# Squared-ReLU MLP of a two-layer decoder: half-width weight loads in the first pass, a third raw tile, and one ring of result tiles

## The chip, the core and the metric

The kernel runs on one core of a Trainium2 chip. The core has a matrix engine (TensorE, PE), whose weight loads are a stream of their own (PEld), a vector engine (VectorE, DVE), a scalar engine (ScalarE, ACT), a general engine (GpSimd, POOL) and a queue engine (SyncE, SP) that here only issues loads. Operands lie in SBUF, 128 partitions wide; PE writes its sums into PSUM banks of 128 x 512 floats. Every engine takes its own instructions strictly in program order and waits on semaphores for what other engines or transfers have to deliver. The metric is the device time of one execution in microseconds (us), less is better. "L76" is line 76 of the kernel of before; where a line of the changed kernel is meant, the text says so.

## The reference

A residual stream of 1024 tokens by 1024 features passes two layers: a token mixer (layer 0 latent attention, layer 1 a gated linear recurrence), then an MLP, all in 32-bit floats. The change touches the first matrix product of the MLP alone, `h @ w1`, and the squared ReLU behind it:

```python
def sq_relu_mlp(h, w1, w2):          # h (1024, 1024), w1 (1024, 4096), w2 (4096, 1024)
    a = jax.nn.relu(h @ w1)
    return (a * a) @ w2

for layer in range(DEPTH):           # DEPTH = 2
    ...
    h = h + rms_norm(m, norm_gains[layer, 1])
    a = rms_norm(h, norm_gains[layer, 2])
    h = h + rms_norm(sq_relu_mlp(a, mlp_w1[layer], mlp_w2[layer]), norm_gains[layer, 3])
```

## The kernel before, in words

**Numbers in two halves.** A 32-bit operand is kept as a rounded high part and the rest. `split` (L74 to L77) makes them: ACT copies the high part (L76), then DVE subtracts it from the source (L77). `mm3` (L79 to L83) multiplies two such operands with three matmuls: high by high, high by low, low by high.

**The product in 16 pairs.** `mlp_up` (L703 to L871) treats `h @ w1` as a product of 2 x 2 blocks with seven block products instead of eight, and additions before and after. The stream h lies in SBUF as four quarters, B11, B12, B21 and B22, of 512 features by 512 tokens each. The 4096 columns of w1 fall into 16 pairs p of 256 columns; a pair has two halves of 128 columns, and each of them an upper and a lower half of the 1024 rows. One block product is 4 x 3 = 12 matmuls of 128 x 512 into one PSUM bank. The seven products of a pair are:

- `first_two` (L787): the first columns' upper rows by B11, copied by ACT to the tile sP1 (L793)
- `add_second` (L796): the first columns' lower rows by B21, added in the same bank; ReLU and square on ACT (L784, L785) make the result h11
- `others` (L803): the five products with T2 (into the bank `tr`), T1 (bank `mm`), T3 (bank `c`), B22 (added to the T1 bank) and T4 (added to the T3 bank). T1 to T4 are sums and differences of the quarters of h, made by `tsums` (L722). Their weights are sums of the raw halves, which DVE makes (L806 to L810) and which are then split. Out of the banks DVE builds U = b + sP1 (L814), X5 (L821), h22, h12, h21 (L825, L828, L831), and after ReLU and square four more sums (L836 to L846)

Seven planes of results per pair are stored to the scratch `hsp` in DRAM by POOL's queue (`spill`, L781). The second matrix product, `mlp_down`, reads them from there.

**Two passes.** A first pass runs `first_two` and `add_second` alone for pairs 0 to 7 (EARLY = 8), while the last rows of the token mixer are still being finished: these two products need only B11 and B21, the others need the sums T1 to T4 of all quarters. `tc.high_priority` (L850) sets where the pass's instructions stand in each engine's order. It stores sP1 to the scratch `psp` (L853) and h11 to plane 0 of `hsp`. The main pass (L860) then loads both back for pairs 0 to 7 (L864, L866) and runs the five products left; for pairs 8 to 15 it runs all seven. One MLP half per layer, so all of this occurs twice.

**Loads.** `raw_half` (L767) brings a 128 x 4 x 256 piece of w1, the upper or the lower rows of both columns of a pair, 512 KB, into a raw tile, on SP's queue. Two raw tiles exist, one in the pool G0 and one in G, taken in turn by the count `own["n"]`. `w_parts` (L772) splits a raw piece or a sum into one of five weight tiles: every fifth by the count `own["w"]` is in G0, four are in G. In the first pass, each piece is loaded in full, and only its first 128 columns are split and used.

**Result tiles.** A 128 x 512 result takes one tile. In the first pass sP1 and h11 take two tiles `he` in G in turn. In the main pass `h512` (L761) gives out tiles: even draws from a ring `h` (9 tiles in layer 0, 6 in layer 1), odd draws from a ring `h2` (4 and 8) in a pool that is opened at L859. A pair draws eight; a tile is reused when its last reader, mostly the store, is done with it.

**Order.** The engines' orders are fixed before the run by a scheduler that places the instructions by priority and readiness; names like raw_920 carry running numbers of the tiles.

Of the kernel before, what the change touches and what calls it, by code (L numbers as in the profile page):

```python
# [11 lines left out]
F32 = mybir.dt.float32  # L12
# [9 lines left out]
P = 128  # L22
# [36 lines left out]
def trunk(ctx, tc, x, x_t, positions, norm_gains, mla_w_in, mla_q_norm, mla_kv_norm, mla_w_uq, mla_w_ukv, mla_w_o,  # L59
# [9 lines left out]
    def new(p, shape, dt, tag, bufs=None):  # L69
        uid[0] += 1  # L70
        kw = {} if bufs is None else {"bufs": bufs}
        return p.tile(shape, dt, tag=tag, name=f"{tag}_{uid[0]}", **kw)
# [630 lines left out]
    def mlp_up(layer):  # L703
# [3 lines left out]
        w1 = mlp_w1[layer].rearrange("(k p) c -> p k c", p=P)  # L707
        with tc.tile_pool(name=f"up{layer}", bufs=1, side="left", reuse_waits="tile") as wp:

            new(wp, [P, 512], F32, "h", 9 if layer == 0 else 6)  # L710
            new(wp, [P, 1024], F32, "s", 3)
            T2 = new(wp, [P, 2, 4, 512], F32R, "T2")
            T3 = new(wp, [P, 2, 4, 512], F32R, "T3")
            T4 = new(wp, [P, 2, 4, 512], F32R, "T4")

            B11, B12, B21, B22 = A[0, 0], A["whole"], A[1, 0], A[1, 1]
            T1 = A[0, 1] if (0, 1) in A else new(wp, [P, 2, 4, 512], F32R, "T1")
# [37 lines left out]
                for k in range(4):  # L755
                    mm3(ps, (w[:, 0, k], w[:, 1, k]), (X[:, 0, k], X[:, 1, k]), not more and k == 0, k == 3, more)

            hs = {"n": 0, "more": None}

            def h512():  # L760
                hs["n"] += 1  # L761
                if hs["more"] and hs["n"] % 2:
                    return new(hs["more"], [P, 512], F32, "h2", 4 if layer == 0 else 8)
                return new(wp, [P, 512], F32, "h", 9 if layer == 0 else 6)

            def raw_half(p, kh):
                own["n"] += 1  # L767
                r = new(G0 if own["n"] % 2 else G, [P, 1024], F32, "raw").rearrange("p (k c) -> p k c", c=256)
                SP.dma_start(r, w1[:, kh * 4:(kh + 1) * 4, p * 256:(p + 1) * 256])
                return r  # L770

            def w_parts(src):  # L772
                own["w"] = own.get("w", 0) + 1
                w = new(G0, [P, 2, 1024], F32R, "w", 1) if own["w"] % 5 == 0 else new(G, [P, 2, 1024], F32R, "w", 4)
                n = src.shape[1] * src.shape[2]
                v = w[:, :, :n].rearrange("p i (k c) -> p i k c", c=src.shape[2])
                split(v, src)
                return v
# [5 lines left out]
                ACT.activation(h, src, AF.Relu)  # L784
                ACT.activation(h, h, AF.Square)  # L785

            def first_two(p, rA, w12):  # L787

                wa = w_parts(rA[:, :, :P])
                a = new(PG, [P, 512], F32, "mm")  # L790
                product(a, wa, B11)
                sP1 = h512() if p >= EARLY else new(G, [P, 512], F32, "he", 2)
                ACT.activation(sP1, a, AF.Copy)  # L793
                return a, sP1
# [53 lines left out]

            for p in range(EARLY):
                with tc.high_priority(offset=AHEAD[layer]):  # L850
                    rA, rB = raw_half(p, 0), raw_half(p, 1)
                    a, sP1 = first_two(p, rA, None)
                    POOL.dma_start(psp[p * P:(p + 1) * P, :], sP1)  # L853
                    wb = w_parts(rB[:, :, :P])
                    add_second(p, a, wb)
            tsums()

            act["whole"].close()
# [1 line left out]
            for p in range(NP):  # L860
                rA, rB = raw_half(p, 0), raw_half(p, 1)
                if p < EARLY:
                    h11 = h512()
                    SP.dma_start(h11, hsp[0, p * P:(p + 1) * P, :])  # L864
                    sP1 = h512()
                    SP.dma_start(sP1, psp[p * P:(p + 1) * P, :])  # L866
                    others(p, rA, rB, w_parts(rB[:, :, P:]), sP1, h11)
                else:
                    a, sP1 = first_two(p, rA, None)
                    wb = w_parts(rB)  # L870
                    others(p, rA, rB, wb[:, :, :, P:], sP1, None, lambda: add_second(p, a, wb))  # L871

# [484 lines left out]
```

## Time and profile before

| | |
|---|---|
| median of 3 runs | 2400.32 us (2399.58 to 2401.26) |
| the profiled execution, its own time | 2396.59 us |
| its span, first to last instruction | 2394.9 us |
| mean granted clock of TensorE | 0.987 |
| mean DMA rate | 143 GB/s (341.51 MB) |
| ReLU of h11 out of the bank (L784, he<-mm) | 16 times, median 597 ns |

The span is that of one execution taken by the profiler; its own time has a little more around the span, and the median of the other runs lies 3.7 us above it. In the profile, a name is the tile that an instruction writes or reads: `raw` a piece of w1 as loaded, `w` a weight tile after the split, `s` a sum, `he`, `h`, `h2` the result tiles, `mm`, `tr`, `c` PSUM banks, `A` the quarters of h, `T` the tiles T1 to T4. A group's row gives line, engine, operation, out<-in with partitions x elements, the count, then busy time and mean nanoseconds of one, then the idle time of its engine just before, with what ended it. A row of the timeline gives start (us from the span's start), duration, engine, line and operation, and in brackets how long the engine had waited and for whom. A row of DMA issues gives the count, the size of one and the median time from issue to landing. In layer 0 the first pass lies at 480 to 545 us and pairs 0 to 7 of the main pass at 545 to 666; in layer 1 at 1720 to 1786 and 1786 to 1916.

### The profile page before, as it was taken

What the parts mean: (1) busy time and instruction counts of PE and PEld (TensorE: products, weight loads), DVE (VectorE), ACT (ScalarE), POOL (GpSimd) and SP (SyncE); (2) the same over time, 40 slices, a digit from 0 to 9 for tenths busy, and PEclk for the clock granted to TensorE, in tenths of its full rate; (3) what the DMA queues carried; (4) which work ended last, traced back from release to release, by engine and by line L of the source; (5) the groups of instructions that cost most, each with busy time, mean ns of one, the idle gap of its engine ahead of it and who ended that gap; (6) DMA issues with size and microseconds to landing.
All of it is one profiled execution on the core that took longest, in us unless ns stands there. A gap on an engine that the chain in (4) does not pass through costs nothing. (4 is left out here: it accounts for less than half of the span.)

```text
span 2394.9 us, 30791 instructions
## 1 busy us (share of the span) xinstructions
PE 2285.7 (95%) x11487; PEld 1918.8 (80%) x11487; DVE 1616.4 (67%) x2311; ACT 1170.9 (49%) x1908; POOL 355.5 (15%) x718
## 2 busy tenths in 40 slices
PE   9999999988899999998899999999978999999996
PEld 8889998866688878886788888888766788888885
DVE  5657884477676557578765667756777767467578
ACT  5445654363344454433575546754453445443443
POOL 1300000121121200001332213221211212100002
PEclk9999999999999999999999999999999999999998
DMA  6000002485554584554612333222455545663743
GB/s 216 27 27 10 10 10 90 157 267 164 172 184 151 187 299 133 190 181 149 219 45 88 106 105 116 83 77 80 150 184 187 200 149 172 214 238 132 257 138 141
DMA packets 229540, 341.51 MB, mean 143 GB/s; under 512 B 16999, under 2 KB 136846, under 8 KB 229390
## 3 DMA queue, kind: packets, MB, share of 16 engines
q1 hardware_dynamic: 205582, 259.84, 33.7%
q0 software_dynamic: 23808, 79.71, 9.0%
q8 instruction: 90, 1.47, 0.3%
q14 instruction: 60, 0.49, 0.1%
HBM read 255.61 MB, written 83.89 MB: 142 GB/s over the span
## 5 line engine op out<-in xcount | busy, mean ns | idle before, releaser
L77 DVE TENSOR_TENSOR w<-raw,w 128x1024 fp32r<-128x1024 f32 (+1 forms) x256 | 280.7, 1102 | 175.9 <-ACT w L76 174.9
L76 ACT ACTIVATE w<-raw 128x1024 fp32r<-128x1024 f32 (+1 forms) x256 | 240.7, 947 | 248.0 <-PE mm L83 82.1
L81 PE MATMUL mm<-A,w 128*128 128x512 f32 x832 | 330.9, 400 | 30.5 <-ACT he L784 12.8
L82 PE MATMUL mm<-A,w 128*128 128x512 f32 x832 | 329.7, 397 | 0.6 <-DVE A L77 0.5
L83 PE MATMUL mm<-A,w 128*128 128x512 f32 x832 | 327.9, 396 | 0.5 <-DVE w L77 0.5
L76 ACT ACTIVATE w<-s 128x1024 fp32r<-128x1024 f32 x156 | 165.1, 1058 | 318.6 <-PE c L83 107.0
L77 DVE TENSOR_TENSOR w<-s,w 128x1024 fp32r<-128x1024 f32 x156 | 190.6, 1222 | 143.2 <-ACT w L76 142.7
L81 PEld LDWEIGHTS mm<-A,w 128*128 128x128 f32 x832 | 158.4, 191 | 72.5 <-ACT he L784 16.1
L145 POOL TENSOR_TENSOR rstd<-rstd,nhalf 128x1 f32<-128x1 f32 x56 | 56.3, 1008 | 964.9 <-DVE rstd L144 939.0
L83 PEld LDWEIGHTS mm<-A,w 128*128 128x128 f32 x832 | 158.7, 191 | 34.2 <-DVE w L77 1.0
L82 PEld LDWEIGHTS mm<-A,w 128*128 128x128 f32 x832 | 158.4, 190 | 33.0 <-DVE A L77 1.4
L82 PE MATMUL mm<-w,w 128*128 128x512 f32 x432 | 171.0, 396 | 12.2 <-DVE w L77 12.2
L781 POOL DMA_DIRECT2D hsp<-h x208 | 112.1, 540 | 467.2 <-ACT h L785 242.6
L83 PE MATMUL mm<-w,w 128*128 128x512 f32 x432 | 169.6, 394 | 0.0
L81 PE MATMUL mm<-w,w 128*128 128x512 f32 x432 | 154.9, 394 | 4.1 <-DVE y L1004 3.2
L81 PE MATMUL mm<-w,A 128*128 128x256 f32 (+2 forms) x352 | 111.1, 318 | 3.6 <-ACT A L76 3.4
L784 ACT ACTIVATE h<-h 128x512 f32<-128x512 f32 x96 | 60.2, 627 | 109.2 <-DVE h L825 70.9
L83 PE MATMUL mm<-w,A 128*128 128x256 f32 (+2 forms) x352 | 111.0, 317 | 0.0
L82 PE MATMUL mm<-w,A 128*128 128x256 f32 (+2 forms) x352 | 110.7, 316 | 0.0
L82 PEld LDWEIGHTS mm<-w,w 128*128 128x128 f32 x432 | 82.1, 190 | 31.2 <-DVE w L77 14.3
L81 PEld LDWEIGHTS mm<-w,w 128*128 128x128 f32 x432 | 81.4, 189 | 24.8 <-ACT w L76 5.7
L81 PE MATMUL c<-T,w 128*128 128x512 f32 x256 | 99.7, 390 | 1.6 <-DVE h L825 1.6
(415 smaller groups left out, 5705.0 us busy)
## 6 DMA issues: line engine op xcount, KB each, us to landing
raw<-in_mlp_w_dram SPq DMA_DIRECT2D x108, 512.0 KB, 4.2
hsp<-h POOLq DMA_DIRECT2D x208, 256.0 KB, 3.1
s<-in_mlp_w_dram SPq DMA_DIRECT2D x80, 512.0 KB, 5.5
raw<-hsp SPq DMA_DIRECT2D x76, 512.0 KB, 4.1
raw<-in_hgrn_w_in_dram SPq DMA_DIRECT2D x64, 512.0 KB, 4.1
sx<-hsp SPq DMA_DIRECT2D x36, 512.0 KB, 4.2
res<-xt POOLq DMA_DIRECT2D x20, 512.0 KB, 4.1
xt<-in_x_dram SPq DMA_DIRECT2D x16, 512.0 KB, 5.7
```

The lines of the kernel that those rows point to most:

```text
L76: ACT.activation(dst[:, 0], src, AF.Copy)
L77: DVE.tensor_tensor(dst[:, 1], src, dst[:, 0].bitcast(F32), ALU.subtract)
L81: PE.matmul(ps, lhs[0], rhs[0], start=start, stop=False, skip_group_check=more)
L82: PE.matmul(ps, lhs[0], rhs[1], start=False, stop=False, skip_group_check=more)
L83: PE.matmul(ps, lhs[1], rhs[0], start=False, stop=stop, skip_group_check=more)
L145: POOL.tensor_tensor(r, r, nhalf[:, :1], ALU.pow)
L781: POOL.dma_start(hsp[i, p * P:(p + 1) * P, :], h)
L784: ACT.activation(h, src, AF.Relu)
```

## The change

1. In the first pass a new function `raw_early` loads only the first 128 columns of a pair, all 1024 rows (128 x 8 x 128, 512 KB in runs of 512 bytes), once per pair where two pieces of 512 KB with runs of 1 KB were loaded. One split of 1024 columns takes the place of two of 512; `first_two` takes the weight tile instead of the raw piece.
2. A third raw tile stands in the pool of `mlp_up`. The main pass takes the three in turn by a count of its own, `hs["r"]`; the first pass takes the old two in turn.
3. `h512` draws from one ring in turn over three pools: the two `he` tiles of the first pass, NH tiles `h` and NM tiles `h2`. In layer 0 NH, NM are 7 and 4 (9 and 4 before), in layer 1 4 and 8 (6 and 8 before): the two `h` tiles less make room for the raw tile.

```diff
+            NH, NM = (7, 4) if layer == 0 else (4, 8)
-            new(wp, [P, 512], F32, "h", 9 if layer == 0 else 6)
+            new(wp, [P, 512], F32, "h", NH)
...
+            new(wp, [P, 1024], F32, "raw")
...
-            hs = {"n": 0, "more": None}
+            hs = {"n": 0, "more": None, "r": 0}
+
+            ring = ["he"] * 2 + ["h"] * NH + ["h2"] * NM
 
             def h512():
+                tag = ring[hs["n"] % len(ring)]
                 hs["n"] += 1
-                if hs["more"] and hs["n"] % 2:
-                    return new(hs["more"], [P, 512], F32, "h2", 4 if layer == 0 else 8)
-                return new(wp, [P, 512], F32, "h", 9 if layer == 0 else 6)
+                p, bufs = {"he": (G, 2), "h": (wp, NH), "h2": (hs["more"], NM)}[tag]
+                return new(p, [P, 512], F32, tag, bufs)
+
+            def raw_early(p):
+
+                own["n"] += 1
+                r = new(G0 if own["n"] % 2 else G, [P, 1024], F32, "raw").rearrange("p (k c) -> p k c", c=P)
+                SP.dma_start(r, w1[:, :, p * 256:p * 256 + P])
+                return r
 
             def raw_half(p, kh):
-                own["n"] += 1
-                r = new(G0 if own["n"] % 2 else G, [P, 1024], F32, "raw").rearrange("p (k c) -> p k c", c=256)
+                hs["r"] += 1
+                r = new((wp, G0, G)[hs["r"] % 3], [P, 1024], F32, "raw").rearrange("p (k c) -> p k c", c=256)
                 SP.dma_start(r, w1[:, kh * 4:(kh + 1) * 4, p * 256:(p + 1) * 256])
                 return r
...
-            def first_two(p, rA, w12):
-
-                wa = w_parts(rA[:, :, :P])
+            def first_two(p, wa):
+
                 a = new(PG, [P, 512], F32, "mm")
                 product(a, wa, B11)
...
             for p in range(EARLY):
                 with tc.high_priority(offset=AHEAD[layer]):
-                    rA, rB = raw_half(p, 0), raw_half(p, 1)
-                    a, sP1 = first_two(p, rA, None)
+                    w12 = w_parts(raw_early(p))
+                    a, sP1 = first_two(p, w12[:, :, :4])
                     POOL.dma_start(psp[p * P:(p + 1) * P, :], sP1)
-                    wb = w_parts(rB[:, :, :P])
-                    add_second(p, a, wb)
+                    add_second(p, a, w12[:, :, 4:])
...
-                    a, sP1 = first_two(p, rA, None)
+                    a, sP1 = first_two(p, w_parts(rA[:, :, :P]))
```

**The queue of loads.** On SP, at the end of layer 0's first pass and the start of the main pass, before: raw_900 to raw_908 are the last two pairs of the first pass, raw_920 and raw_921 are pair 0 of the main pass, raw_938 and raw_939 pair 1, raw_956 and raw_957 pair 2; the rows from psp and hsp are pair 0's sP1 and h11.

```order
L769 DMA raw_900_5331<-in_mlp_w1_dram 128x4x256
L866 DMA h_923_5463<-psp_851_5069 128x512
L769 DMA raw_901_5333<-in_mlp_w1_dram 128x4x256
L769 DMA raw_907_5373<-in_mlp_w1_dram 128x4x256
L769 DMA raw_908_5375<-in_mlp_w1_dram 128x4x256
L769 DMA raw_920_5457<-in_mlp_w1_dram 128x4x256
L769 DMA raw_921_5459<-in_mlp_w1_dram 128x4x256
L864 DMA h2_922_5461<-hsp_850_5068 128x512
L769 DMA raw_938_5570<-in_mlp_w1_dram 128x4x256
L769 DMA raw_939_5572<-in_mlp_w1_dram 128x4x256
```

The same place in the changed program, by its own line numbers: L774 is `raw_early`, L780 `raw_half`, L873 and L875 the loads of h11 and sP1. Pair 0 is raw_905 and raw_906, pair 1 is raw_923 and raw_924, pair 2 begins with raw_941.

```order
L774 DMA raw_889_5302<-in_mlp_w1_dram 128x8x128
L774 DMA raw_894_5339<-in_mlp_w1_dram 128x8x128
L780 DMA raw_905_5418<-in_mlp_w1_dram 128x4x256
L780 DMA raw_923_5531<-in_mlp_w1_dram 128x4x256
L780 DMA raw_906_5420<-in_mlp_w1_dram 128x4x256
L875 DMA h2_926_5537<-psp_851_5069 128x512
L873 DMA he_907_5422<-hsp_850_5068 128x512
L780 DMA raw_924_5533<-in_mlp_w1_dram 128x4x256
L780 DMA raw_941_5644<-in_mlp_w1_dram 128x4x256
L875 DMA he_908_5424<-psp_851_5069 128x512
L780 DMA raw_942_5646<-in_mlp_w1_dram 128x4x256
```

Pair 1's first half now stands ahead of pair 0's second, and pair 0's sP1, which stood ahead of all of the main pass's raw loads, now stands behind pair 2's first half and goes to an `he` tile.

**ACT at the end of the first pass.** In layer 0 before: he_906 and he_913 are h11 of the last two pairs, he_911 is sP1 of the last, T3 and T4 are splits of `tsums`, w_927 is the split of the weight sums for the main pass's first product, w_930 that for the T3 product.

```order
L784 ACTIVATE he_906_5369<-mm_903_5338 128x512
L793 ACTIVATE he_911_5393<-mm_910_5380 128x512
L785 ACTIVATE he_906_5369<-he_906_5369 128x512
L76 ACTIVATE T3_855_5076<-s_917_5434 128x1024
L784 ACTIVATE he_913_5411<-mm_910_5380 128x512
L785 ACTIVATE he_913_5411<-he_913_5411 128x512
L76 ACTIVATE w_927_5472<-s_925_5468 128x1024
L76 ACTIVATE T4_856_5077<-s_919_5436 128x1024
```

The same steps in the changed program; he_893 and he_898 are h11 of the last two pairs, he_897 is sP1, w_912 is the split for the main pass's first product.

```order
L795 ACTIVATE he_893_5335<-mm_891_5307 128x512
L803 ACTIVATE he_897_5357<-mm_896_5344 128x512
L796 ACTIVATE he_893_5335<-he_893_5335 128x512
L76 ACTIVATE T3_855_5076<-s_902_5395 128x1024
L76 ACTIVATE w_912_5433<-s_910_5429 128x1024
L795 ACTIVATE he_898_5372<-mm_896_5344 128x512
L796 ACTIVATE he_898_5372<-he_898_5372 128x512
L76 ACTIVATE T4_856_5077<-s_904_5397 128x1024
```

The split w_912 has moved ahead of the last pair's ReLU and square. In layer 1 the changed order at this place is ReLU, square, T3, then the split.

**DVE at the third pair.** In layer 0 before: L806 makes the first sum of pair 3 out of its two raw halves raw_974 and raw_975, and L77 with s_961 is the split of pair 2's sums, which PE needs for pair 2's T2 product.

```order
L836 TENSOR_TENSOR h_935_5558<-h_932_5508,h2_934_5523 128x512
L839 TENSOR_TENSOR h2_936_5561<-h_935_5558,h2_922_5461 128x512
L842 TENSOR_TENSOR h_932_5508<-h2_922_5461,h_932_5508 128x512
L831 TENSOR_TENSOR h2_929_5490<-c_933_5510,h2_929_5490 128x512
L806 TENSOR_TENSOR s_979_5807<-raw_974_5796,raw_975_5798 128x4x128
L77 TENSOR_TENSOR w_963_5698<-s_961_5694,w_963_5698 128x1024
L807 TENSOR_TENSOR s_979_5807<-s_979_5807,raw_974_5796 128x4x128
```

In the changed program pair 3's sum is L816 out of raw_959 and raw_960, and pair 2's split is that of s_946; L846, L849, L852 and L841 are what L836, L839, L842 and L831 were.

```order
L846 TENSOR_TENSOR h_920_5519<-h_917_5469,h_919_5484 128x512
L816 TENSOR_TENSOR s_964_5768<-raw_959_5757,raw_960_5759 128x4x128
L849 TENSOR_TENSOR h_921_5522<-h_920_5519,he_907_5422 128x512
L852 TENSOR_TENSOR h_917_5469<-he_907_5422,h_917_5469 128x512
L817 TENSOR_TENSOR s_964_5768<-s_964_5768,raw_959_5757 128x4x128
L841 TENSOR_TENSOR h_914_5451<-c_918_5471,h_914_5451 128x512
L77 TENSOR_TENSOR w_948_5659<-s_946_5655,w_948_5659 128x1024
```

Pair 3's first sum still stands ahead of pair 2's split, now by six rows instead of one.

## The prediction

> **What bounds the kernel now.** I read the totals of the page first, then the windows of the up stages, then what TensorE (PE) waited for in them.
>
> ```profile
> span 2394.9 us, 30791 instructions
> PE 2285.7 (95%) x11487; PEld 1918.8 (80%) x11487; DVE 1616.4 (67%) x2311; ACT 1170.9 (49%) x1908; POOL 355.5 (15%) x718
> 480.00:545.00 65.00, 52.18 (x228) 40.47 (x228) 52.81 (x63) 39.23 (x69) 13.08 (x24) 0.97 0.76 251
> 545.00:666.00 121.00, 106.42 (x434) 83.82 (x435) 82.13 (x117) 45.17 (x62) 19.93 (x37) 0.96 0.55 177
> 666.00:790.00 124.00, 124.00 (x548) 102.68 (x547) 84.73 (x118) 61.32 (x88) 26.43 (x49) 1.00 0.48 165
> 1720.00:1786.00 66.00, 52.92 (x225) 41.08 (x224) 52.27 (x62) 38.75 (x72) 16.82 (x26) 0.95 0.67 219
> 1786.00:1916.00 130.00, 118.10 (x494) 94.06 (x495) 93.76 (x133) 53.14 (x72) 23.16 (x43) 0.97 0.56 188
> 1916.00:2090.00 174.00, 173.69 (x765) 143.21 (x764) 106.12 (x141) 83.30 (x120) 33.44 (x62) 1.00 0.51 172
> ```
>
> The rows give a window, its length, then the busy time of PE, weight loads, DVE, ACT and POOL, the granted clock, the DMA share and GB/s. PE is the bound. Pairs 8 to 15 run without a gap, one matmul every 124.00 / 548 = 0.226 us. By that pace the two windows of pairs 0 to 7 need 434 x 0.226 = 98.1 and 494 x 0.226 = 111.6 us; they take 121 and 130, an excess of **22.9 and 18.4 us**. In the two first passes PE stands idle for 65 - 52.2 = 12.8 and 66 - 52.9 = 13.1 us. Only these four windows, some 67 us plus the half clock of the first passes, can give anything; an edit that acts elsewhere is worth nothing.
>
> **The change part by part.** *First pass, halved loads.* Each pair loses one 512 KB load and trades two splits of 512 columns for one of 1024.
>
> ```profile
> L76 ACT ACTIVATE w<-raw 128x512 fp32r<-128x512 f32 x14 | 8.9, 634 | 13.9 <-DMA raw<-in_mlp_w_dram 10.7 <-PE mm L83 3.2
> L76 ACT ACTIVATE T<-s 128x1024 fp32r<-128x1024 f32 x7 | 7.3, 1055 | 1.8 <-DVE s L739 0.9 <-DVE s L742 0.6 <-DVE s L745 0.2
> L77 DVE TENSOR_TENSOR w<-raw,w 128x512 fp32r<-128x512 f32 x15 | 10.3, 686 | 6.1 <-ACT w L76 6.1
> L77 DVE TENSOR_TENSOR T<-s,T 128x1024 fp32r<-128x1024 f32 x7 | 8.4, 1218 | 0.1
> raw<-in_mlp_w_dram SPq DMA_DIRECT2D x108, 512.0 KB, 4.2
> raw<-in_hgrn_w_in_dram SPq DMA_DIRECT2D x64, 512.0 KB, 4.1
> ```
>
> Over 16 pairs ACT saves 16 x (2 x 634 - 1055) = 3.4 us and DVE 16 x (2 x 686 - 1218) = 2.5 us. I credit 0: ACT is busy 39 of 65 us here and PE's products cover it; without that cover it is at most 5.9. The first product now needs a split of 1055 ns on ACT where 634 did, 0.4 us later if the split came just in time; ACT's order puts it two pairs ahead, so 0. The new load has runs of 512 bytes where the old has 1 KB; the HGRN projection's loads, most of them the same 128x8x128, land in 4.1 us against 4.2, so a load costs the same, and eight fewer are in a layer's queue. The Trainium skill, "DMA: Bandwidth & Descriptors", section "Why small descriptors are slow (HBM only)", gives a fixed 3 cycles per packet beside one per 32 bytes; by that an estimate is 19 cycles per 512 bytes against 35 per 1 KB, 9% slower, some 0.4 us a load. The two rows do not show it.
>
> What counts is whom the loads held up. ACT takes its work in order, and stood at a split for a raw half with the release of a PSUM bank (L784) behind it:
>
> ```profile
> 1748.77 1.15 ACT L76 ACTIVATE w<-raw 128x512 fp32r<-128x512 f32 x2 [4.44 <-DMA raw<-in_mlp_w_dram]
> 1758.13 1.15 ACT L76 ACTIVATE w<-raw 128x512 fp32r<-128x512 f32 x2 [2.14 <-DMA raw<-in_mlp_w_dram]
> 482.27 0.63 ACT L76 ACTIVATE w<-raw 128x512 fp32r<-128x512 f32 x1 [2.20 <-DMA raw<-in_mlp_w_dram]
> 1750.46 0.51 PE L81 MATMUL mm<-A,w 128*128 128x512 f32 x1 [2.70 <-ACT he L784]
> 1759.82 0.50 PE L81 MATMUL mm<-A,w 128*128 128x512 f32 x1 [2.03 <-ACT he L784]
> 483.44 0.73 PE L81 MATMUL mm<-A,w 128*128 128x512 f32 x2 [1.83 <-ACT A L76]
> 499.60 0.49 PE L81 MATMUL mm<-A,w 128*128 128x512 f32 x1 [1.08 <-ACT he L793]
> PE mm L81 <- ACT he L784: 6.0, 5, 2.0
> 1750.00:1754.00 4.00, 3.54 (x9) 2.85 (x10) 2.80 (x5) 2.38 (x5) 1.12 (x2) 0.60 0.67 187
> 1761.00:1765.00 4.00, 4.00 (x13) 3.13 (x12) 4.00 (x4) 1.78 (x2) 0.61 (x2) 0.57 0.87 270
> 484.00:488.00 4.00, 3.89 (x10) 2.97 (x10) 3.76 (x5) 1.39 (x2) 0.55 (x1) 0.57 1.08 381
> ```
>
> One raw tile now carries a whole pair, so two tiles run two pairs ahead instead of one. Five waits for L784 in layer 0 sum to 6.0 us, 1.2 each: two PSUM banks in turn, with the same PE order in the new program, so about 1.2 us per pair stays. Layer 1: the 2.70 goes, 2.03 falls to 1.2, and the half-clock stretches behind them (0.40 x 4 and 0.43 x 4 = 3.3) go: 6.8, I take **6**. Layer 0: 1.83 falls by 1.2, the half clock by 1.7, the 1.08 goes, since the copy L793 of pair 1 moves up in ACT's row: **4**.
>
> *The start of the main pass.* Here the new buffer order adds a wait. Pair 0 takes its h11 and sP1 in the two he tiles, which the last pairs of the first pass still hold: their stores must land first. In layer 0:
>
> ```profile
> 545.01 0.54 POOL L781 DMA_DIRECT2D hsp<-he  x1 [3.38 <-ACT he L785]
> DMA to landing us min/median/max: 2.3/2.5/2.6
> h<-psp SPq DMA_DIRECT2D x16, 256.0 KB, 4.7
> hsp<-he POOLq DMA_DIRECT2D x16, 256.0 KB, 4.9
> 545.72 0.66 PE L81 MATMUL tr<-T,w 128*128 128x512 f32 x1 [2.34 <-ACT w L76]
> 1787.38 0.50 PE L81 MATMUL tr<-T,w 128*128 128x512 f32 x1 [2.34 <-ACT w L76]
> 1799.72 0.50 PE L81 MATMUL mm<-A,w 128*128 128x512 f32 x1 [2.09 <-DVE h L821]
> ```
>
> PE's last product of the pass ended at 545.72 - 2.34 = 543.38, and the last store left 1.6 us later. Its landing takes 2.5 (the second row, stores of 536 to 550 us) and the load of sP1 4.7, so U of pair 0 can be made 1.6 + 2.5 + 4.7 = 8.8 us after the pass, and X5 (L821, now L831) about 2 us later, three DVE steps on. PE has products of 36 x 0.226 = 8.1 us to do meanwhile, then needs X5. Behind the waiting load on SP stand the raw loads of pair 1 (layer 1) or pair 2 (layer 0); the first step of these pairs' sums on DVE waits for them. In layer 0 ACT's row puts pair 0's split ahead of the last ReLU, so the 2.34 goes and most of it comes back as this wait: **1** gained. In layer 1 a T3 split stands ahead of it (1 us more), while 2.09 is there already: **0**. Ends for both layers together: all gaps of these rows gone, 6.8 gained; or nothing hidden, 2 x (8.8 - 8.1 + 2) = 5.4 lost. I stay near the middle, as the wait overlaps what is there.
>
> *The third raw tile.* DVE works in order too. It stood at the sum L806 of the pair after next until its raw landed, with the split that PE needed behind it:
>
> ```profile
> 572.24 0.69 DVE L806 TENSOR_TENSOR s<-raw,raw 128x512 f32<-128x512 f32 x1 [3.98 <-DMA raw<-in_mlp_w_dram]
> 572.85 1.22 DVE L77 TENSOR_TENSOR w<-s,w 128x1024 fp32r<-128x1024 f32 x1
> 574.12 0.80 PE L83 MATMUL tr<-T,w 128*128 128x512 f32 x1 [3.27 <-DVE w L77]
> 574.00:580.00 6.00, 5.88 (x14) 4.63 (x15) 5.06 (x9) 0.75 (x2) 0.54 (x1) 0.50 0.64 201
> 1817.74 0.50 PE L83 MATMUL tr<-T,w 128*128 128x512 f32 x1 [3.17 <-DVE w L77]
> 1817.00:1823.00 6.00, 5.26 (x16) 4.22 (x17) 5.67 (x9) 0.15 (x1) 0.54 (x1) 0.72 0.60 196
> DVE s L806 <- DMA raw<-in_mlp_w_dram: 18.3, 6, 4.4
> DVE h L814 <- DMA h<-psp: 8.2, 3, 4.1
> ```
>
> With three tiles a pair's first half is there before the pair ahead ends, and its second half is asked for at the last read of the *first* half ahead (L809), one to four DVE steps of 0.69 us before that of the second (L810). Walking the new rows of SP and DVE from the end of the first pass: pair 1's second half is asked for at 2 us and lands at 6.3; pair 1's sums have read its first half at 9, so pair 2's second half lands at 13.3; pair 2's first half is read at 16.5, behind results of pair 0, and pair 3's second half lands at 21. Pair 3's sum starts there, not at 572.24 - 543.38 = 28.9, and the split for pair 2 stands complete before PE asks for it. Both gaps go, with the half clock behind them: 3.27 + 0.50 x 6 = **6** and 3.17 + 0.28 x 6, **5**.
>
> *Result tiles in one ring.* A pair takes eight. Before, odd and even draws came from two rings (4 beside 9, 8 beside 6), so a tile came back after 8 and 12 draws; now after 13 and 14. So the loads of h11 and sP1 wait for stores of two pairs back, not one, and most of the 8.2 us at L814 goes. Of the excess left in pairs 0 to 7 (22.9 less 6 and about 2.4 of the start: 14; 18.4 less 5 and about 5: 8) other DVE steps behind L806 and L814 hold most. I take somewhat over half: **8 and 4**. Ends: nothing, or all 22.
>
> *Shifted counters.* The weight tiles' count moves on by 64 per layer instead of 72, so the five tiles take other turns later; all five are alike, and the raw tiles' alternation keeps its parity: 0. Downstream, PE is without gaps; if that cover broke, one gap like the above would cost 3.
>
> **Sum.** 6 + 4 + 1 + 0 + 6 + 5 + 8 + 4 = 34 us off the profiled execution's 2396.6, so 2362.6. The median of the runs shown, 2400.3, lies 3.7 above it: **2366**.
>
> **The rivals.** *The new wait takes the place of the old* (0.20): first passes and the third pair's gaps improve, but U of pair 0 holds PE and the ring's loads block raw loads on SP, so the 12 of the small stalls do not come and the start costs 5 to 6: 34 - 12 - 6 = 16, about 2384. For it: one SP queue in order; against: loads were late by raw tiles, not by SP. *The half clock stays* (0.08): 3.3 + 1.7 + 3.0 + 1.7 = 9.7 of the sum is clock that the rows charge behind gaps of 1.8 to 3.3 us; if it falls behind the gaps of about 1.2 that remain too, 34 - 9.7 = 24 and 2376. Against it: 0.50 stands right behind 3.27. The Trainium skill, "TensorE: Matmul & The Clock Gate", section "HAM oscillation — how this bites in real kernels", asks only for no idle gaps over about 3.4 us; by that rule no gap here would halve the clock and closing them would not give it back. The rows disagree. *More than forecast* (0.11): all small stalls and the start go, 22 + 6.8 + 21, about 2350. *No change* (0.06): raw loads come earlier, but a bank, a weight tile or a store holds each step where it was, within 5 us, 2400; this is also the case in which the edit does not get its loads ahead. *Slower* (0.06): the stores from the he tiles land late (4.9 us is their median on the page) and PE has nothing to do beside the wait, so each layer loses the whole 1.6 + 4.9 + 4.7 + 2 = 13 at its start and some 3 to half clock behind it, against a gain of the first passes and layer 0's third pair alone, 6 + 4 + 6: 2400 + 32 - 16 = 2416. It decides when that wait costs PE over 8 us in each layer beyond what its 8.1 us of products cover.
>
> **How the numbers follow.** The forecast's case has 0.49, from 2356 to 2376. To leave out no more than 0.2 the range takes in both neighbours: below, the end with nearly all excess gone, 2347; above, the gaps of the first passes and layer 0's third pair alone with the start's cost half paid, 2390. Faster by over 0.2% (4.8 us, about what a measurement here can tell from no change) 0.88, within 0.06, slower 0.06.
>
> **What would show it.** Right: no wait of ACT on a raw load over 2 us in the first passes; no gap of PE near 3 us and no clock of 0.50 at the third pair; L814 (now L824) waiting for sP1 once per layer, at pair 0, with PE idle 1 to 3 us before the product that follows X5. Wrong: such waits at every pair, SP's raw loads issued late behind h loads, or new gaps in pairs 8 to 15. What would upset the forecast most is a clock that falls to half at the start of the main pass although its gaps are short.

## The result and the profile after

The changed kernel takes 2379.83 us (median of 4 runs, 2378.43 to 2383.45) against 2400.79 us of the kernel before in the same session: a ratio of **0.9911, 95% interval 0.9893 to 0.9929**, 21 us less. The forecast was 2366, 34 us less: the gain came out at 0.6 of it, within the range.

The totals of the changed kernel's page:

```profile
span 2377.4 us, 30721 instructions
PE 2282.1 (96%) x11487; PEld 1920.7 (81%) x11487; DVE 1613.7 (68%) x2295; ACT 1169.6 (49%) x1893; POOL 355.8 (15%) x718
```

PE's busy time is 3.6 us less for the same 11,487 matmuls, and the rest of the 17.5 us by which the span is shorter is idle time of PE. The kernel before had a profiled execution 4 us faster than its median; hence 17.5 here and 21 between the medians.

Windows of the changed kernel over pairs 0 to 7: window, its length, busy time of PE, weight loads, DVE, ACT and POOL with counts, granted clock, DMA share, GB/s. The first is the stretch shown of layer 0 before; the second is 130 us from the start of layer 1's main pass, whose stretch before began 1.4 us ahead of that start.

```profile
545.00:666.00 121.00, 116.96 (x512) 95.82 (x512) 95.56 (x137) 54.54 (x76) 23.64 (x44) 1.00 0.64 214
1772.00:1902.00 130.00, 125.53 (x534) 102.21 (x535) 99.97 (x143) 56.49 (x79) 25.21 (x47) 0.97 0.61 202
```

In layer 0, PE does 512 matmuls where it did 434, at full clock: 78 x 0.226 = 17.6 us of work more in the same stretch. In layer 1 it does 534 where it did 494, 9.0 us.

To see where time went over the whole program, I cut both traces at seven places that every version has, in the same order of work. Grouped rows of the kernel before (count; shortest, median and longest duration; first and last start):

```profile
L689 ACT ACTIVATE y<-mm x8: 594/598/622, 443.1 to 499.4; 128x512 f32<-128x512 f32 x8
L1002 ACT ACTIVATE y<-mm x16: 579/598/601, 872.3 to 2218.0; 128x512 f32<-128x512 f32 x16
L1252 PE MATMUL c<-kT,q x96: 270/275/377, 1222.8 to 1699.1; 128*128 128x128 f32 x96
```

The same rows of the changed kernel, whose lines behind the edit are 9 higher:

```profile
L689 ACT ACTIVATE y<-mm x8: 593/600/627, 443.7 to 501.2; 128x512 f32<-128x512 f32 x8
L1011 ACT ACTIVATE y<-mm x16: 598/599/601, 854.4 to 2197.8; 128x512 f32<-128x512 f32 x16
L1261 PE MATMUL c<-kT,q x96: 270/275/377, 1204.3 to 1683.8; 128*128 128x128 f32 x96
```

The first start of L689 lies ahead of the first pass of layer 0; the first and the last of L1002 lie in the second matrix product of layers 0 and 1; the last of L1252 is near the end of layer 1's mixer. With the first product with T2 in each main pass (545.72 and 1787.38 before) and the end of the span they make six stages. The two starts in the changed kernel, in its timeline (start, duration, what it is, idle time before it and its releaser):

```profile
543.14 0.39 PE L81 MATMUL tr<-T,w 128*128 128x512 f32 x1
1771.97 0.79 PE L81 MATMUL tr<-T,w 128*128 128x512 f32 x1 [5.37 <-ACT w L76]
```

| stage, us | before | changed | difference | forecast |
|---|---|---|---|---|
| first pass, layer 0 | 102.6 | 99.5 | -3.1 | -4 |
| main pass, layer 0 | 326.6 | 311.2 | **-15.4** | -15 |
| from there to the end of layer 1's mixer | 826.8 | 829.4 | **+2.6** | 0 |
| first pass, layer 1 | 88.3 | 88.2 | **-0.1** | -6 |
| main pass, layer 1 | 430.6 | 425.8 | -4.8 | -9 |
| last stage | 176.9 | 179.6 | **+2.7** | 0 |

(The start lies 0.6 us later in the changed kernel: 18.1 - 0.6 = 17.5.) So layer 0 came out near the forecast. Three things did not: layer 1's first pass gained nothing, its main pass half, and 5.3 us were lost in stages whose work the change does not touch.

Two things limit this table. PE's wait ahead of the first product with T2 lies before the cut, so in the first pass's stage: 2.34 us before in both layers, none and 5.37 us in the changed kernel. Without it the first passes took 100.3 and 99.5 us in layer 0, 85.9 and 82.8 in layer 1, a gain of 0.8 and 3.1. And each column is one profiled execution; executions of one kernel spread by up to 13 us (2388.85 to 2401.83 in one of the runs below), so a difference of a few us in one stage counts only where other runs show it too.

### The profile page after: what moved, and what is told of

The parts are those of the page before. It is cut to its first block, busy times and chain, and to the rows that moved or that the text cites. A ratio compares the mean times of both kernels' runs of the same rounds, so it can differ in the third digit from the quotient of the medians.

```text
span 2377.4 us, 30721 instructions
## 1 busy us (share of the span) xinstructions
PE 2282.1 (96%) x11487; PEld 1920.7 (81%) x11487; DVE 1613.7 (68%) x2295; ACT 1169.6 (49%) x1893; POOL 355.8 (15%) x718
## 5 line engine op out<-in xcount | busy, mean ns | idle before, releaser
L77 DVE TENSOR_TENSOR w<-raw,w 128x1024 fp32r<-128x1024 f32 (+1 forms) x240 | 278.9, 1167 | 191.1 <-ACT w L76 190.2
L81 PE MATMUL mm<-A,w 128*128 128x512 f32 x832 | 330.9, 399 | 21.4 <-ACT he L795 12.1
L77 DVE TENSOR_TENSOR w<-s,w 128x1024 fp32r<-128x1024 f32 x156 | 190.5, 1222 | 152.4 <-ACT w L76 152.4
L82 PE MATMUL mm<-w,w 128*128 128x512 f32 x432 | 170.9, 396 | 10.7 <-DVE w L77 10.7
L792 POOL DMA_DIRECT2D hsp<-h x177 | 95.3, 539 | 387.6 <-ACT h L796 207.2
L81 PE MATMUL c<-T,w 128*128 128x512 f32 x256 | 99.6, 389 | 0.0
L82 PE MATMUL c<-T,w 128*128 128x512 f32 x256 | 99.6, 389 | 0.0
```

The lines of the kernel that those rows point to most:

```text
L77: DVE.tensor_tensor(dst[:, 1], src, dst[:, 0].bitcast(F32), ALU.subtract)
L81: PE.matmul(ps, lhs[0], rhs[0], start=start, stop=False, skip_group_check=more)
L82: PE.matmul(ps, lhs[0], rhs[1], start=False, stop=False, skip_group_check=more)
L792: POOL.dma_start(hsp[i, p * P:(p + 1) * P, :], h)
```

## The experiments

Each ran with the kernel before on the same chip, which took 2399 to 2401 us there. Where an edit says "old turns", the count of the weight tiles is moved on so that behind the first pass the tiles are taken in turn as before the change.

### The turns of the weight tiles

The changed kernel with the old turns:

```diff
             tsums()
+            own["w"] += 8
```

> The changed kernel, with the count of the weight tiles moved on by 8 after each first pass, so that behind it the five weight tiles take the turns they had before the change. Theory 1 (turns): the changed turns altered the scheduler's order at the seam from layer 0 to layer 1 and in the last rows, and that order cost some 3 us at the seam and 5 us at the end; with the old turns both come back, so 8 to 12 us faster than the changed kernel's 2379.8, about 2370, and the gaps of PE behind the last gather of results are those of before. Theory 2 (a later wait): PE arrives earlier there and meets work of DVE and ACT that did not move; the turns do not matter, so 2378 to 2382.

Measured: 2372.3 us (2369.17 to 2378.73), ratio **0.9888** (0.9872 to 0.9905), 7.5 us less than the changed kernel, where theory 1 had 8 to 12; the intervals of the two ratios overlap, the spans are 2367.5 and 2377.4. The last stage took 176.9 us instead of 179.6 and the one from layer 0's main pass to the end of layer 1's mixer 824.9 instead of 829.4, as theory 1 says.

The kernel before, with the turns that the changed kernel has:

```diff
             tsums()
+            own["w"] += 2
```

> The kernel of before, with nothing changed but the count of the weight tiles, moved on by 2 after each first pass, so that the tiles take the turns of the changed kernel behind it. Theory 1 (turns): the seam and the last rows lose what they lost in the changed kernel, 5 to 10 us: 2406 to 2411 against 2400.8. Theory 2 (a later wait): five equal tiles in other turns cost nothing: 2399 to 2403.

Measured: 2402.3 us (2395.27 to 2404.47), 1.0005 (0.9994 to 1.0017). By the median theory 2 holds. In the trace the last stage took 179.5 us instead of 176.9, the stage between 832.3 instead of 826.8 and the main pass of layer 1 435.7 instead of 430.6, while the main pass of layer 0 and the first pass of layer 1 came out 3.3 and 3.8 us shorter. These do not cancel: the two profiled executions lie 7.2 us apart, the medians 1.7, so the sizes are uncertain by some us. The loss in the last stage comes back in every run with other turns (below).

What the turns do at the end shows in the last rows of the changed kernel, DVE then PE:

```profile
2340.18 1.21 DVE L77 TENSOR_TENSOR w<-sx,w 128x1024 fp32r<-128x1024 f32 x1
2341.32 1.22 DVE L966 TENSOR_TENSOR s<-s,s 128x1024 f32<-128x1024 f32 x1
2342.45 1.28 DVE L1013 TENSOR_TENSOR y<-mm,y 128x512 f32<-128x512 f32 x2
2343.28 0.77 PE L81 MATMUL mm<-wx,w 128*128 128x512 f32 x1 [2.74 <-DVE y L1013]
2344.00:2350.00 6.00, 6.00 (x17) 4.70 (x16) 6.00 (x8) 4.34 (x10) 0.00 (x0) 0.55 0.50 205
```

DVE makes a split and a sum ahead of L1013, which gives back the bank that PE needs. PE waits 2.74 us and then runs 6 us at 0.55 of its clock. The same place with the old turns:

```profile
2331.82 1.22 DVE L967 TENSOR_TENSOR s<-s,s 128x1024 f32<-128x1024 f32 x1
2332.95 1.28 DVE L1014 TENSOR_TENSOR y<-mm,y 128x512 f32<-128x512 f32 x2
2333.78 0.47 PE L81 MATMUL mm<-wx,w 128*128 128x512 f32 x1 [0.45 <-DVE y L1014]
2334.00:2340.00 6.00, 6.00 (x27) 4.93 (x27) 6.00 (x9) 4.58 (x11) 0.00 (x0) 1.00 0.75 255
```

The split of `sx` now comes behind the bank's release, the wait is 0.45 and the clock stays at 1.00. In the kernel before with the changed turns the wait is there again, of the same length, and the window from 2368.8 to 2374.8 us has a clock of 0.56:

```profile
2368.07 0.77 PE L81 MATMUL mm<-wx,w 128*128 128x512 f32 x1 [2.74 <-DVE y L1005]
```

At this product PE waits 2.74 to 4.43 us in all six kernels with other turns, and at most 0.5 us in all eight with the old ones. So five equal tiles in other turns are not worth 0. They alter which tile comes free when, and the scheduler writes another order. The old turns have a price of their own at another place, where the second product of layer 0 begins: PE waits 3.51 us there, which the changed kernel does not.

```profile
821.04 0.73 PE L81 MATMUL mm<-w,w 128*128 128x512 f32 x2 [3.51 <-ACT w L76]
```

### How much is order alone

Two more turns, each for the kernel before and for the changed one, to see how far equal work in another order moves the time, and whether the gain depends on it.

```diff
             tsums()
+            own["w"] += 1
```

and, in the changed kernel,

```diff
             tsums()
+            own["w"] += 9
```

> The kernel of before with nothing changed but the turns of the weight tiles (their count moved on by 1 after each first pass). It asks how much another order of equal work moves the time by itself. Theory 1 (the buffers gain, the order adds a few us either way): 2394 to 2407. Theory 2 (before is an unlucky order, and any edit that shakes it up gains some 15 to 20): 2380 to 2388.

> The changed kernel with the same turns of the weight tiles as the run before this one (count moved on by 9). Theory 1: 20 to 30 us faster than the kernel of before in the same turns, 2370 to 2382. Theory 2: less than 10 faster than it.

Measured: 2394.74 us (0.9982, 0.9970 to 0.9994) and 2377.87 us (0.9912, 0.9897 to 0.9928), 16.9 us apart.

Then `+= 3` in the kernel before and `+= 11` in the changed one, at the same place.

> As the first, with the count moved on by 3. Theory 1: 2394 to 2407. Theory 2: 2380 to 2388.

> The changed kernel in the turns of the run before this one (count moved on by 11). Theory 1: 20 to 30 us faster than that run, 2370 to 2382. Theory 2: less than 10 faster.

Measured: 2399.41 us (0.9996, 0.9985 to 1.0007) and 2390.37 us (0.9963, 0.9948 to 0.9977), **9.0 us** apart. Neither theory holds as it stands. No order of the kernel before gains 15 us, as theory 2 had it; the four lie between 2394.7 and 2402.3. But theory 1's 20 to 30 us were missed in both pairs, and 9.0 is within theory 2's "less than 10". The two other turns gave 28.3 us (the old ones) and 22.5 (the changed kernel against the kernel before in its turns, run in two sessions). The change gains in every order, and the order decides how much.

Stage by stage, the changed kernel less the kernel before in the same turns (in us; one profiled execution each; that of the changed kernel in the last column lay 8 us above its median):

| stage | forecast | old turns | the changed kernel's | moved on by 1 | moved on by 3 |
|---|---|---|---|---|---|
| first pass, layer 0 | -4 | -5.6 | -4.2 | -4.2 | -3.1 |
| main pass, layer 0 | -15 | **-11.9** | **-12.0** | **-13.4** | **-11.4** |
| from there to the end of layer 1's mixer | 0 | -1.9 | -2.9 | -2.9 | +3.5 |
| first pass, layer 1 | -6 | -1.6 | +3.7 | +4.3 | +4.2 |
| main pass, layer 1 | -9 | -5.7 | -9.9 | -6.6 | +4.4 |
| last stage | 0 | 0.0 | +0.1 | +3.3 | +0.4 |

Layer 0's main pass gains 11 to 13 us in every order: this part belongs to the change and not to the order. The 15.4 us of the first table hold some 3 us that the turns alone gave there. Layer 1 is where the order decides.

### The three parts

The halved loads alone (two raw tiles, old rings, old turns):

```diff
-                    rA, rB = raw_half(p, 0), raw_half(p, 1)
+                    w12 = w_parts(raw_early(p))
...
+            own["w"] += 8
```

> The halved loads of the first pass alone: two raw tiles, the old rings of result tiles, the old turns of the weight tiles. Theory 1 (moved wait): in layer 1 the first pass ends 3 to 4 us earlier, but the main pass starts when DVE has made the sums T1 to T4, which does not move, so little is left: 2397 to 2401. The forecast's reading: 4 us in layer 0 and 6 in layer 1, so 2391.

Measured: **2380.51 us**, 0.9921 (0.9909 to 0.9933): 20 us, where the forecast's reading gave 10 and the other theory 4 at most. Both are wrong on the sum. The first pass of layer 1 did not gain (91.1 us against 88.3), but the main pass of layer 0 took 315.2 us instead of 326.6, with two raw tiles.

The third raw tile alone (full loads, old turns, the old rings with two h tiles less; the first pass keeps the old two raw tiles):

```diff
-            new(wp, [P, 512], F32, "h", 9 if layer == 0 else 6)
+            new(wp, [P, 512], F32, "h", NH)
+            new(wp, [P, 1024], F32, "raw")
...
-                r = new(G0 if own["n"] % 2 else G, [P, 1024], F32, "raw").rearrange("p (k c) -> p k c", c=256)
+                r = new((wp, G0, G)[hs["r"] % 3], [P, 1024], F32, "raw").rearrange("p (k c) -> p k c", c=256)
```

> The third raw tile alone: the first pass with two loads a pair, the two old rings of result tiles (7 and 4, 4 and 8), the old turns. Theory 1 (the ring gives nothing): 2376 to 2380, as the third raw tile with the ring (2377.4). The forecast's reading: 11 us from the third pair's stalls alone, about 2390.

Measured: 2382.88 us, 0.9926 (0.9913 to 0.9940), between the two expectations.

The one ring alone (two raw tiles, full loads, old turns):

```diff
+            ring = ["he"] * 2 + ["h"] * NH + ["h2"] * NM
...
-                if hs["more"] and hs["n"] % 2:
-                    return new(hs["more"], [P, 512], F32, "h2", 4 if layer == 0 else 8)
-                return new(wp, [P, 512], F32, "h", 9 if layer == 0 else 6)
+                p, bufs = {"he": (G, 2), "h": (wp, NH), "h2": (hs["more"], NM)}[tag]
+                return new(p, [P, 512], F32, tag, bufs)
```

> The one ring of result tiles alone (he 2, h 9 or 6, h2 4 or 8), with two raw tiles, two loads a pair in the first pass, the old turns. Theory 1 (the ring gives nothing): 2398 to 2402. The forecast's reading: 8 + 4 less the new wait at the start, about 2390. Theory 3 (the wait of pair 0's results for the he tiles costs without the third raw tile's slack): 2403 to 2410.

Measured: **2378.20 us**, 0.9907 (0.9893 to 0.9920), 21 us. All three expectations miss; the ring alone gives as much as either other part, its interval overlapping theirs.

Third raw tile and ring, with full loads (old turns), and halved loads and third raw tile, with the old rings (old turns). The edits are those above, two at a time.

> The third raw tile and the one ring of result tiles, with the first pass as before (two loads of 512 KB a pair) and the old turns of the weight tiles. Theory 1 (main pass alone): the gains of pairs 0 to 7, about 18 us in layer 0 and 9 in layer 1 in the changed kernel's trace, come from these two edits: 2400.8 - 25 = about 2376, not slower than the changed kernel, with the first passes as before. Theory 2 (the halved loads carry it): the main pass gains because the queue of loads is shorter ahead of it, so without the halved loads pairs 1 to 3 wait again and half of the 27 us is lost: about 2388.

> Halved loads and third raw tile with the old turns of the weight tiles, but the result tiles from the two old rings (odd and even draws; 7 and 4 tiles in layer 0, 4 and 8 in layer 1). Theory 1 (the raw loads were the only limit in pairs 0 to 7; the ring of result tiles gives nothing): within 2 us of the 2372.3 that the same kernel with the one ring took. The forecast's reading (the ring gives 12 us over both layers): about 2384.

Measured: 2377.36 us, 0.9908 (0.9895 to 0.9921), and 2372.37 us, 0.9888 (0.9873 to 0.9903). The first confirms that the main pass can gain without the halved loads. The second is level with all three parts together (2372.3): beside the other two, the ring adds nothing that these runs can tell.

So the parts give 20.1, 16.3 and 21.0 us alone, 57 in sum, and 28.3 together in the same turns. They are not three separate gains. The waits of DVE and PE in the 121 us from 545 to 666 us of layer 0 show why (us in total, times, longest; both engines). The changed kernel:

```profile
DVE s L816 <- DMA raw<-in_mlp_w_dram: 6.3, 6, 2.0
DVE h L824 <- DMA h<-psp: 3.4, 3, 1.8
PE tr L83 <- DVE w L77: 1.0, 1, 1.0
```

The ring alone:

```profile
DVE s L809 <- DMA raw<-in_mlp_w_dram: 16.9, 8, 5.4
DVE h L817 <- DMA h<-psp: 4.9, 3, 2.3
PE tr L83 <- DVE w L77: 2.1, 2, 1.8
```

The halved loads alone:

```profile
DVE s L813 <- DMA raw<-in_mlp_w_dram: 16.1, 7, 3.4
DVE h L821 <- DMA h<-psp: 4.4, 3, 2.4
PE tr L83 <- DVE w L77: 1.2, 2, 0.8
```

The kernel before had 18.3 us for the raw tiles, 8.2 for sP1, and PE's waits for DVE's split were 5.0, the longest 3.3. With either part alone DVE still stands at the raw loads for 16 to 17 us, with two raw tiles as before, but all of PE's waits in this window sum to 7.0 us with the ring and 5.7 with the halved loads, where they were 16.1 before and are 3.6 in the changed kernel. So it is not the time that DVE waits for loads that decided. My reading is that it was what stood behind that wait on DVE, and whether the wait for sP1 came on top. A pair costs DVE 14 x 0.69 + 2 x 1.22 = 12.1 us by the durations; but the next step starts 0.61 or 1.14 us after one starts (1743.29 and 1743.90, 2340.18 and 2341.32 in rows of this text), so in a row they take 14 x 0.61 + 2 x 1.14 = 10.8 us, beside PE's 60 x 0.226 = 13.6. With under 3 us to spare, two waits in one pair may reach PE where one does not. That each part takes away about as much is measured; why the ring does so as well as the raw tile was not tried apart.

### The first pass of layer 1

The changed kernel with the old turns, and the first pass drawing its results from the he and the h tiles in turn:

```diff
-                sP1 = h512() if p >= EARLY else new(G, [P, 512], F32, "he", 2)
+                sP1 = h512() if p >= EARLY else early512()
...
+            def early512():
+                tag = ring[hs["e"] % (2 + NH)]
+                hs["e"] += 1
+                p, bufs = {"he": (G, 2), "h": (wp, NH)}[tag]
+                return new(p, [P, 512], F32, tag, bufs)
```

> The changed kernel with the old turns, and the first pass draws its results from the he tiles and the h tiles in one ring (9 tiles in layer 0, 6 in layer 1) instead of the two he tiles. Theory 1 (in layer 1's first pass ACT stands at the copy of the next sP1 until the store out of its he tile has landed, up to 2.1 us, and DVE behind it): these waits go, DVE's hole of 6.7 us ahead of the sums T shrinks by about 2, the main pass starts 2 to 3 us earlier: 2368 to 2370 against 2372.3. Theory 2 (PE's two banks set the pace of the first pass): the waits turn into waits for the bank, 2371 to 2374.

Measured: 2376.36 us (2372.16 to 2379.14), 0.9903 (0.9887 to 0.9920). No gain over 2372.3, and above both expectations; the intervals overlap. The first pass of layer 1 did fall, from 86.7 to 84.0 us, and DVE's hole, its idle time ahead of the sums T, from 6.7 to 1.9. But the order changed as well. On PE, 132 of the 192 matmuls of the first pass now come behind the last transposes of the mixer's rows, instead of 84 in layer 1 and 108 in layer 0; so PE stands at those transposes until the rows are normed, with work queued behind them. The longest such waits, in layer 0 and in layer 1:

```profile
506.63 1.94 PE L176 MATMUL tr<-ident,y 128*128 128x128 f32 x8 [4.89 <-issue]
1738.12 1.94 PE L176 MATMUL tr<-ident,acc 128*128 128x128 f32 x8 [5.16 <-DVE acc L204]
```

Layer 0's first pass took 104.8 us instead of 97.0. This run changes tiles and order at once, so alone it does not tell which of them closed DVE's hole; the orders of all runs, below, speak for the order.

The same stages over all runs that bear on the first passes:

| first pass, us | layer 0 | layer 1 |
|---|---|---|
| full loads (before, its three other turns, ring alone, third raw tile alone, both) | 101.8 to 104.8, mean 103.3 | 83.1 to 88.3, mean 85.2 |
| halved loads and two he tiles (changed, its three other turns, halves alone, halves and third raw tile) | 97.0 to 101.7, mean 99.3 | 86.2 to 91.1, mean 88.3 |

In layer 0 the halved loads gain 4.0 us, in layer 1 they **cost 3.1**. Three pairs of kernels in the old turns differ in the loads alone (halves alone against before, halves and third raw tile against the raw tile alone, all parts against raw tile and ring): -5.0, -1.9 and -7.8 us in layer 0, +2.9, +0.4 and +3.6 in layer 1. In layer 0, 2.3 us of the gain are the wait at the start of the main pass, which is 2.34 to 2.52 us in all seven kernels with full loads and is gone in all six others.

## Why the prediction was right, and where not

**First pass, layer 0 (4): near in size, by luck.** 3.1 in the changed kernel, 4.0 in the mean of six against seven runs; but 2.3 of it is the wait at the start of the main pass, which the forecast counted under the start, so 0.8 and 1.7 are left. ACT's waits for raw loads fell as forecast, from 10.7 us to 2.1. PE's waits for the release of a bank did not, 8.3 us before and 9.0 in the changed kernel; so the step from an earlier load to an earlier bank failed here too. The two rows of before, of which the forecast showed the first, and those of the changed kernel:

```profile
PE mm L81 <- ACT he L784: 6.0, 5, 2.0
PE mm L81 <- ACT he L793: 2.3, 2, 1.2
PE mm L81 <- ACT he L795: 5.7, 6, 1.9
PE mm L81 <- ACT he L803: 3.3, 2, 2.1
```

**First pass, layer 1 ("I take 6"): wrong.** The argument was that a load of ACT's split holds up the release of a bank. The loads did come earlier: ACT's waits for them fell from 13.1 us in seven waits to 4.2 in two. But PE's waits for a bank stayed, 8.0 us before and 7.6 in the changed kernel (the longest, 2.58 us, behind a split of ACT that waited for DVE, with a clock of 0.52 behind it, where the forecast had the 2.70 and its half clock gone). And PE is not all that the main pass waits for: its first product needs the sums that DVE makes, and these need the last quarter of h, which ACT copies at L178 after PE has transposed it. The path from the last norm (L204) to that product in the kernel before:

```profile
1745.26 1.28 DVE L204 SCALAR_TENSOR_TENSOR acc<-xt,rstd,gpre 128x1024 f32<-128x1024 f32 x1 [0.74 <-POOL rstd L145]
1746.69 1.06 PE L176 MATMUL tr<-ident,acc 128*128 128x128 f32 x8 [1.11 <-DVE acc L204]
1751.30 0.60 ACT L178 ACTIVATE acc<-tr 128x512 f32<-128x512 f32 x1
1783.66 0.69 DVE L807 TENSOR_TENSOR s<-s,raw 128x512 f32<-128x512 f32 x1
1785.12 0.60 ACT L784 ACTIVATE he<-mm 128x512 f32<-128x512 f32 x1 [1.73 <-PE mm L83]
1786.29 1.04 ACT L76 ACTIVATE w<-s 128x1024 fp32r<-128x1024 f32 x1
```

DVE's last sum (L807) ends at 1784.35, and ACT splits it 1.9 us later, because the ReLU behind PE's last product comes first. So PE's gaps could give no more than these 1.9 us, unless DVE's sums came earlier as well. The same path in the changed kernel:

```profile
1731.38 1.28 DVE L204 SCALAR_TENSOR_TENSOR acc<-xt,rstd,gpre 128x1024 f32<-128x1024 f32 x1 [0.76 <-POOL rstd L145]
1739.24 1.03 PE L176 MATMUL tr<-ident,acc 128*128 128x128 f32 x8
1742.14 0.60 ACT L803 ACTIVATE he<-mm 128x512 f32<-128x512 f32 x1 [2.06 <-DMA hsp<-he]
1743.16 0.59 ACT L178 ACTIVATE acc<-tr 128x512 f32<-128x512 f32 x1
1743.29 0.69 DVE L77 TENSOR_TENSOR w<-raw,w 128x512 fp32r<-128x512 f32 x1 [7.00 <-ACT w L76]
1743.90 1.22 DVE L740 TENSOR_TENSOR s<-acc,A 128x1024 f32<-128x1024 f32 x1
1770.86 1.06 ACT L76 ACTIVATE w<-s 128x1024 fp32r<-128x1024 f32 x1 [1.28 <-DVE s L817]
```

The row is normed at 1732.66, but PE comes to its transposes only 6.6 us later, where it took 0.15 before: 24 more products of the first pass stand ahead of them in PE's order (84 of the 192 are left behind them, 108 before). The copy L803 ahead of L178 then waits 2.06 us for a store to leave its he tile. From the norm to L178 it takes 10.5 us instead of 4.8, and DVE stands idle for 7.00. From L178 to the T2 product it takes 28.8 us instead of 36.1, DVE's sums nearly without a gap, and PE waits 5.37 us at the end, for ACT's split of DVE's sum. So 7.3 us are gained behind L178, and 5.7 are lost between the norm and L178 and 1.4 ahead of the norm. A hole of DVE of 4.4 to 7.0 us is in each of the six kernels with halved loads and two he tiles: PE leaves 84 products (96 in one) behind the transposes and comes to them 4.8 to 6.7 us after the norm. In the seven with full loads it leaves 106 to 108 and comes 0.1 to 1.1 us after it, and no hole at this place is over 2.9; with 132 left, in the run above, it is 1.9. No run moved these products alone, so that the order makes the hole is shown by this agreement and not by an edit. The step that failed is to price PE's gaps "with the same PE order in the new program": the order was another, and behind PE's gaps stood DVE's sums.

**Start of the main pass (1 and 0).** The wait that the forecast feared, of pair 0's U for its he tile, did not come; the DVE row of layer 0 has no idle time ahead of it:

```profile
552.75 0.68 DVE L824 TENSOR_TENSOR h<-tr,he 128x512 f32<-128x512 f32 x1
```

So layer 0's start gave the whole 2.3 us. In layer 1 the start waits 5.37 us where it waited 2.34, for the sums, as above.

**Third pair and ring, layer 0 (6 + 8): near in sum, wrong as a sum.** The gap of 3.27 us and its half clock are gone, and 15.4 us came where 15 were forecast, the start's 1 among them; in equal turns it is 11 to 13, so the close match is in part luck. And the terms are not separate: each part alone takes 7 to 11 us off this stage (from 326.6 to 319.5, 315.2 and 315.2), two of them 12 to 13, and all three 8 to 17 in the four turns.

**Third pair and ring, layer 1 (5 + 4): half in this order.** The stage gave 4.8; in equal turns it gave 5.7, 9.9 and 6.6 us, and lost 4.4 in the fourth, so its size depends on the order. One new gap is at the last pair of the first eight:

```profile
1857.83 1.06 ACT L76 ACTIVATE w<-s 128x1024 fp32r<-128x1024 f32 x1 [2.05 <-PE mm L83]
1860.90 0.47 PE L81 MATMUL tr<-T,w 128*128 128x512 f32 x1 [3.10 <-DVE he L824]
```

ACT waits for PE to be done with a weight tile, DVE's split and U (L824) come behind it, and PE waits for its bank. With the old turns there is no gap of this length here.

**"Shifted counters: 0" and "Downstream, PE is without gaps": wrong.** 5.3 us were lost there (2.6 and 2.7). Over all runs, the last stage takes 176.6 to 177.7 us in the eight kernels with the old turns and 178.6 to 182.3 in the six with others. The single wait with the half clock behind it is shown above for two of them. The 2.6 us of the stage between are less sure: the old turns give 824.2 to 829.4 there, the others 827.8 to 832.3.

**Rivals.** Slower and no change are out. "The half clock stays" (2376) and "the new wait takes the place of the old" (2384) lie 4 us on either side of the measured time, nearer than the forecast, but neither by what it named. U of pair 0 did not hold PE. And behind gaps of 1.0 to 1.4 us that stood alone the clock stayed at 1.00, in the window of 545 to 666 us.

**The sum.** 3.1 + 15.4 + 0.1 + 4.8 instead of 34, less 5.3 downstream. With the turns put back, the same change measures 28.3 us.

## What to carry to other kernels

In a kernel whose order a scheduler writes from the state of its buffers, a change of any buffer's count rewrites the order far behind the edit; here equal work in four orders spread over 8 us before the change and 18 after it, so a gain of 1% should be tried in several such orders before it is credited to the edit, and the best one (here 2372 us) kept. Buffers that feed one in-order engine are not worth a sum of terms: price the loop's slack once (here 10.8 us of DVE beside 13.6 of PE per pair), since the first part takes most of it. And before counting the gaps of the busiest engine in a stage, look for the chain that sets the stage's end, and read in the new order what stands ahead of it on every engine.

## What the hardware showed that was not expected

The new load, with runs of 512 bytes, lands in 5.5 us in the median of layer 0's eight and 4.4 of layer 1's, where the old one took 5.1 and 4.3 in the first passes; the forecast set them equal from another load of that shape. In the seven kernels with full loads these medians scatter from 5.0 to 5.8 us in layer 0 and 4.3 to 6.1 in layer 1, in the six with halved loads from 5.1 to 6.3 and 4.4 to 5.6. The estimate that the prediction worked out from the Trainium skill, "DMA: Bandwidth & Descriptors", section "Why small descriptors are slow (HBM only)", was 0.4 us more a load; these runs neither show it nor rule it out.

A wait of PE of 2.74 us in the last stage was followed by 6 us at 0.55 of the clock. In layer 0's first pass of the changed kernel, two waits of nearly one length, 2.09 and 1.95 us, were followed by different clocks. The two waits, and the windows behind them:

```profile
491.52 0.50 PE L81 MATMUL mm<-A,w 128*128 128x512 f32 x1 [2.09 <-ACT he L803]
520.27 0.50 PE L81 MATMUL mm<-A,w 128*128 128x512 f32 x1 [1.95 <-ACT he L795]
491.50:495.00 3.50, 3.48 (x10) 2.83 (x11) 3.41 (x6) 1.42 (x3) 1.15 (x2) 0.65 0.93 323
520.30:524.00 3.70, 3.70 (x16) 3.05 (x17) 3.17 (x4) 2.65 (x5) 1.08 (x2) 1.00 0.19 73
```

The Trainium skill, "TensorE: Matmul & The Clock Gate", section "HAM oscillation — how this bites in real kernels", asks for no idle gap over about 3.4 us; these rows show the half clock behind shorter ones, and not behind each. What tells the two waits apart is not shown.
